# Gate and up of blocks 4 to 14 of a second feed-forward by seven block products, in a hybrid encoder layer on one core

## The chip, the core and the metric

The kernel runs on one core of one Trainium2 chip. The metric is the device time of one execution in microseconds (us); the number before the change is the median of three runs. Engines are called as in the profile: PE (TensorE matmul), PEld (its weight loads), DVE (VectorE), ACT (ScalarE), POOL (GpSimd), SP (SyncE, which here only issues transfers).

## What is computed

One layer of an encoder on 544 tokens (512 of a prompt and 32 of a sample, D = 1024): a feed-forward half step, a mixing stage (retention and sparse attention), and a second feed-forward half step, each closed by a layer norm on a scaled residual. The part that matters is the second feed-forward:

```python
def swiglu(h, w_gate, w_up, w_down):
    a = jnp.einsum('btd,df->btf', h, w_gate)
    u = jnp.einsum('btd,df->btf', h, w_up)
    return jnp.einsum('btf,fd->btd', jax.nn.silu(a) * u, w_down)
...
x = post_norm(x, swiglu(modulate(x, sh3, sc3), f2_gate, f2_up, f2_down), 1.0 + gt3, 0.5, ln3_g, ln3_b)
```

The hidden width is 2816, which is 22 blocks of 128 columns.

## The kernel before, in words

Everything is held transposed: features on the 128 partitions, tokens along the free axis, in two halves of 272 (`HALVES`). All large products run in fp32r with operands split in a high and a low part; `mm3` (line 140) makes three matmuls of one product of tiles: high by high, high by low, low by high. Each matmul is 128x128 weights by 272 columns, recorded under line 75 (`mm`).

A feed-forward block f (`ffn_up`, line 194) takes one gate and one up weight block of [1024, 128], and for each of them and each half of the tokens runs 8 contraction tiles by 3 matmuls into one PSUM bank (`ffn_mm`): 4 x 24 = 96 matmuls. `ffn_act` then makes tanh on ACT (line 188), the gating and the product on DVE (189, 190), the high part of the hidden block on ACT (191) and the low part on DVE (192). Gate halves use three banks of tag "a", up halves two of "l" and two of "t". Blocks 0 and 1 run side by side, contraction tile by contraction tile (`k_outer`), while the normalised input `h` is still being made; blocks 2 to 21 follow one by one.

Weights flow through a list `stream`, made up ahead by `queue_w`. `next_w` keeps three weights (`AHEAD`) split beyond the one in use. For each, `fetch_w` loads 512 KB on SP into one of three buffers `wr`; `split_w` casts the high part on ACT (line 129) into one of five buffers `wh`, writes its negative to the low part on ACT (133), and POOL issues a transfer that adds the weight from DRAM to it (134). With `lo_eng` given, that engine subtracts instead (136).

The order of issue is set by hand where it matters: all PE instructions, and all loads issued through `load`, are chained in program order. `tick()` is called after each product and resumes jobs that were spawned and asked to be resumed so many ticks later; so side work is put into the program at a pace. `tc.keep_in_program_order` pins an instruction's place; other instructions may be moved ahead by the scheduler when their engine is free. Each engine runs its queue in order. SBUF beside weights is one pool of 35 units (`unit`, 128x1088 floats): `h` takes 8, the hidden blocks 22, the residual `xr` 4, the partial sums and weight tiles of the conditioning products the rest.

Two pieces of side work lie beside the second feed-forward. `residual_next` (355) turns the residual into its scaled form: eight multiplies on POOL (359) and eight scalings on ACT (361), spawned before block 2. `cond((8, (2, 3)))` makes the last gate's conditioning vector on DVE: eight loads of 512 KB and sixteen products over 1024 columns (554, 556), one step every 2 or 3 ticks from block 2 on, then `cond_done`. After block 21 the down projection (`proj_residual`) reads the hidden blocks, adds to the residual, and the last layer norm ends the kernel.

Of the kernel before, what the change touches and what calls it, by code (L numbers as in the profile page):

```python
# [9 lines left out]
F32 = mybir.dt.float32  # L10
FR = mybir.dt.float32r
I32 = mybir.dt.int32
AF = mybir.ActivationFunctionType
ALU = mybir.AluOpType
NOSYNC = mybir.DependencyInfo(mybir.DependencyClass.NoSync, mybir.DependencyReason.DATA)

P = 128
D = 1024
ND = D // P
TP = 512  # L20
TS = 32
T = TP + TS
HT = T // 2
FF = 2816
NF = FF // P
# [5 lines left out]
HALVES = ((0, HT), (HT, T))  # L31
SEGS = ((((0, HT), 0),), (((HT, TP), 0), ((TP, T), 1)))
DOWN_G = ((0, 8), (8, 15), (15, 22))
AHEAD = 3


@with_exitstack
def encoder_layer_kernel(ctx, tc, xT, cT, wc1, w_e, w_cond, b_condT, lnp, w_gu1, w_dn1, w_in, w_out, w_gu2, w_dn2,
                         ckT, cv, cikT, s0, cmat, ropes, dec, csm,
                         yT, akT, avT, ikT, st_p, st_s):  # L40
    nc = tc.nc
    ctx.enter_context(nc.allow_low_precision("operands are split exactly into two float32r parts"))
    const = ctx.enter_context(tc.tile_pool(name="const", bufs=1))
    up = ctx.enter_context(tc.tile_pool(name="up", bufs=35))
    wr = ctx.enter_context(tc.tile_pool(name="wr", bufs=3))
    wh = ctx.enter_context(tc.tile_pool(name="wh", bufs=5))
# [4 lines left out]
    def unit(name, dt=F32):  # L51
        return up.tile([P, 2, T], dt, name=name, tag="u")

    def scr(name, shape=None, dt=F32):
        return sp.tile(shape or [P, T], dt, name=name, tag="s", bufs=4)

    def half_scr(name, shape=None):
        return sp.tile(shape or [P, HT], F32, name=name, tag="t", bufs=4)

    def bank(tag, name):  # L60
        return pp.tile([P, 512], F32, name=name, tag=tag, bufs=dict(a=3, l=2, t=2, o=1)[tag])
# [9 lines left out]
    def load(*a):  # L71
        ordered("load", nc.sync.dma_start(*a))

    def mm(*a, **kw):
        ordered("pe", nc.tensor.matmul(*a, **kw))  # L75
# [14 lines left out]
    def spawn(job):  # L90
        resume(job, now[0] + 1)

    def tick():
        now[0] += 1
        due = [j for t, j in jobs if t <= now[0]]
        jobs[:] = [x for x in jobs if x[0] > now[0]]
        for job in due:
            resume(job, now[0])
# [19 lines left out]
    def fetch_w(src, n, name):  # L118
        raw = wr.tile([P, ND, P], F32, name=f"wr_{name}", tag="wr")
        load(raw[:, :n, :], src)  # L120
        return raw

    def split_w(raw, n, name, lo_eng=None, pool=None, pin=False, src=None):
        if pool is None:
            hl = wh.tile([P, 2, ND, P], FR, name=f"wh_{name}", tag="wh")
            hi, lo = hl[:, 0], hl[:, 1]
        else:
            hi, lo = (pool.tile([P, ND, P], FR, name=f"wu_{name}", tag="u") for _ in range(2))
        c = nc.scalar.copy(hi[:, :n, :], raw[:, :n, :])  # L129
        if pin:  # L130
            tc.keep_in_program_order(c)
        if src is not None and lo_eng is None:
            nc.scalar.mul(lo[:, :n, :], hi[:, :n, :].bitcast(F32), -1.0)  # L133
            nc.gpsimd.dma_start(lo[:, :n, :], src, accum_op=ALU.add)  # L134
        else:
            r = (lo_eng or nc.gpsimd).tensor_tensor(lo[:, :n, :], raw[:, :n, :], hi[:, :n, :].bitcast(F32), op=ALU.subtract)
            last["lo"] = r.ins.name
        return hi, lo
# [7 lines left out]

    stream = []
    split = []

    def ensure(n):  # L150
        while len(split) < n and stream:
            src, cnt, kw = stream.pop(0)
            split.append(split_w(fetch_w(src, cnt, "w"), cnt, "w", src=src, **kw))

    def next_w(ahead=AHEAD):
        ensure(1 + ahead)
        return split.pop(0)

    def queue_w(src, n=ND, **kw):
        stream.append((src, n, kw))  # L160
# [12 lines left out]
    def ffn_mm(st, h, which, i, tag=None):  # L173
        hls, banks = st
        if hls[which] is None:
            hls[which] = next_w()
        a, b = HALVES[i]
        ps = bank(tag or ("a" if which == 0 else "lt"[i]), f"gu{which}_{i}")[:, :HT]
        for k in range(ND):
            mm3(ps, hls[which], k, h[k], a, b, k == 0, k == ND - 1)  # L180
        banks[which, i] = ps
        tick()

    def ffn_act(st, hid, i):
        a, b = HALVES[i]
        pg, pu = st[1][0, i], st[1][1, i]
        t = half_scr("tnh")
        nc.scalar.activation(t, pg, AF.Tanh, scale=0.5)  # L188
        nc.vector.scalar_tensor_tensor(t, t, 1.0, pg, op0=ALU.add, op1=ALU.mult)  # L189
        nc.vector.tensor_tensor(t, t, pu, op=ALU.mult)  # L190
        nc.scalar.copy(hid[:, 0, a:b], t)  # L191
        nc.vector.tensor_tensor(hid[:, 1, a:b], t, hid[:, 0, a:b].bitcast(F32), op=ALU.subtract)  # L192

    def ffn_up(h, hid):
        st = [None, None], {}
        for which in range(2):
            for i in range(2):
                ffn_mm(st, h, which, i)
        for i in range(2):
            ffn_act(st, hid, i)  # L200
# [154 lines left out]
    def residual_next(xr, rs, al, j):  # L355

        for i, (a, b) in enumerate(HALVES):
            rb = rs[i].unsqueeze(1).to_broadcast([P, 2, HT])
            tc.keep_in_program_order(nc.gpsimd.tensor_tensor(xr[j][:, :, a:b], xr[j][:, :, a:b], rb, op=ALU.mult))
        for d in (2 * j, 2 * j + 1):  # L360
            tc.keep_in_program_order(nc.scalar.activation(xv(xr, d), xv(xr, d), AF.Identity, bias=al[1][:, d:d + 1],
                                                          scale=al[0][:, d:d + 1]))
# [32 lines left out]
    DN += [(6, *g, 1) for g in ((8, 12), (12, 15), (15, 18), (18, 22))] + [(7, *g, 1) for g in DOWN_G]  # L395
    OUT = [(d, 0, 8, i) for i in range(2) for d in range(ND)]

    def queue_ffn(w_gu, w_dn, f0, first=False):
        for f in range(f0, NF):
            for which in range(2):  # L400
                queue_w(w_gu[f - f0, which], lo_eng=(nc.gpsimd, nc.vector)[which] if first and f == f0 else None,
                        pin=first and 2 * (f - f0) + which < AHEAD)
        for d in range(ND):
            for k0, k1 in DOWN_G:
                queue_w(w_dn[d][:, k0:k1, :], k1 - k0)

    queue_ffn(w_gu1, w_dn1, 2, True)
    for c in range(4):
        queue_w(w_in[c], lo_eng=nc.gpsimd if c else nc.vector, pool=up)
    for c in [4] + [17 + hh + 4 * j for hh in range(4) for j in range(3)] + [  # L410
# [5 lines left out]
        queue_w(w_gu2[0, which], pool=up)  # L416
    queue_w(w_gu2[1, 0])
    queue_w(w_gu2[1, 1], pool=up)
    queue_ffn(w_gu2[2:], w_dn2, 2)


    xr = [unit(f"xr{j}") for j in range(4)]
    h = new_h("h1_")
# [61 lines left out]
    for d in range(ND):  # L485
# [17 lines left out]
        x = xv(xr, d)  # L503
        for i in range(2):
            a0, b0 = HALVES[i]
            f = half_scr("hf")
            for (a, b), r in SEGS[i]:
                nc.vector.tensor_scalar(f[:, a - a0:b - a0], x[:, a:b], g1[:, r, d:d + 1], modT[:, r, d:d + 1],
                                        op0=ALU.mult, op1=ALU.add)
# [6 lines left out]
    for n in range(len(ACC)):  # L516
        catch_up(n, ND)
    ensure(AHEAD)
    onesr = const.tile([P, P], FR, name="onesr")
# [24 lines left out]
    def cond(*parts):  # L544
        n = 0
        for m, pace in parts:
            acc = [up.tile([P, 1024], F32, name=f"ca{m}_{r}", tag="u") for r in range(2)]
            for d in range(ND):
                w = up.tile([P, 1024], F32, name=f"wc{m}_{d}", tag="u")
                load(w, w_cond[d * P:(d + 1) * P, 1024 * m:1024 * m + 1024])  # L550
                for r in range(2):
                    c = cz[:, d, r:r + 1]
                    if d == 0:
                        nc.vector.tensor_scalar(acc[r], w, c, None, op0=ALU.mult)
                    else:
                        nc.vector.scalar_tensor_tensor(acc[r], w, c, acc[r], op0=ALU.mult, op1=ALU.add)  # L556
                n += 1
                yield pace[n % len(pace)]
            spawn(cond_done(m, acc))
# [11 lines left out]
    hid = []  # L571
# [14 lines left out]
    al2 = alpha_ln(2, lp[:, 2, :], lp[:, 3, :])  # L586
    G2, B2 = mod_consts(2, 3, 4, lp[:, 0, :], lp[:, 1, :])

    h, rs, fin = ln_to_h(xr, G2, B2, "h2_", 4, 1)
# [6 lines left out]
    xd = nc.dram_tensor("x_spill", [4, P, 2 * T], F32, kind="Internal").ap()  # L596
# [547 lines left out]
    for hh in range(4):  # L1144
        mixed[hh] = unit("mx", FR)
        if hh == 0:
            xr = [unit(f"xq{j}") for j in range(4)]
# [4 lines left out]
        def gated(ps, a, b):  # L1152
            t = half_scr("rgt")
            nc.scalar.activation(t, ps, AF.Tanh, scale=0.5)
            nc.vector.scalar_tensor_tensor(t, t, 1.0, ps, op0=ALU.add, op1=ALU.mult)
            nc.vector.tensor_mul(t, t, rt[:, a:b])
            mixed_part(hh, t, a, b)
# [6 lines left out]
    h, rs, fin = ln_to_h(xr, G3, B3, "h3_", 3, 4)  # L1164
# [2 lines left out]

    hid = [unit("hid", FR), unit("hid", FR)]
    sts = [([next_w(0), next_w(0)], {}) for f in range(2)]
    for i in range(2):  # L1170
        for f in range(2):
            for which in range(2):
                sts[f][1][which, i] = bank(("aaao", "lltt")[i][2 * f + which], "gu_e")[:, :HT]
        k_outer([(sts[f][0][w], sts[f][1][w, i]) for f in range(2) for w in range(2)], h, i)
        for f in range(2):
            ffn_act(sts[f], hid[f], i)

    def residual():
        yield 2
        for j in range(4):  # L1180
            residual_next(xr, rs, al2, j)
            yield 1

    spawn(residual())
    for f in range(2, NF):
        hid.append(unit("hid", FR))
        ffn_up(h, hid[f])
        if f == 2:
            spawn(cond((8, (2, 3))))
    known(8)  # L1190
    C3 = gate_coef(3, 8, 0.25)

# [146 lines left out]
```

## Time and profile before

| | |
|---|---|
| median of 3 runs | 1190.45 us (1190.23 to 1190.97) |
| profiled execution | 1189.48 us |
| its span, first to last instruction | 1187.4 us |
| mean granted clock of PE | 0.991 |
| PE busy | 1159.3 us, 98% |
| DVE, ACT, POOL busy | 56%, 49%, 17% |
| matmuls under line 75 of gate and up (both feed-forwards, from block 2) | 3840, 482.7 us |

The second feed-forward's blocks 0 and 1 end at 798.56 us in the span, blocks 2 to 21 at about 1039 us, and the down projection and the norm take the rest. In rows of the profile, `out<-in` are the program's names of what is written and read, the figure behind the count is the busy time in us and the next the mean of one in ns; behind the second bar stands the idle time of the engine ahead of them and what ended it. In rows of the chain and of the timeline the first two numbers are start and length in us.

### The profile page before, as it was taken

What the parts mean: (1) busy time and instruction counts of PE and PEld (TensorE: products, weight loads), DVE (VectorE), ACT (ScalarE), POOL (GpSimd) and SP (SyncE); (2) the same over time, 40 slices, a digit from 0 to 9 for tenths busy, and PEclk for the clock granted to TensorE, in tenths of its full rate; (3) what the DMA queues carried; (4) which work ended last, traced back from release to release, by engine and by line L of the source; (5) the groups of instructions that cost most, each with busy time, mean ns of one, the idle gap of its engine ahead of it and who ended that gap; (6) DMA issues with size and microseconds to landing.
All of it is one profiled execution on the core that took longest, in us unless ns stands there. A gap on an engine that the chain in (4) does not pass through costs nothing.

```text
span 1187.4 us, 23002 instructions
## 1 busy us (share of the span) xinstructions
PE 1159.3 (98%) x9419; PEld 1127.8 (95%) x9419; DVE 665.8 (56%) x1574; ACT 586.7 (49%) x990; POOL 199.7 (17%) x231
## 2 busy tenths in 40 slices
PE   9999999999999999899989999999999999999995
PEld 7999999999999999789979989999999999999995
DVE  5767665764468484677887775885542222201416
ACT  3644444444335364655466577546444444433423
POOL 0112111111111303312111101104111111111110
PEclk9999999999999999999989999999999999999998
DMA  9899999997999466644845588807988878788842
GB/s 359 293 297 308 239 256 229 258 215 183 296 259 215 119 222 168 149 116 115 193 100 162 132 257 225 209 31 197 263 177 175 177 175 173 163 173 176 177 88 76
DMA packets 71451, 231.41 MB, mean 195 GB/s; under 512 B 8657, under 2 KB 12881, under 8 KB 71345
## 3 DMA queue, kind: packets, MB, share of 16 engines
q0 software_dynamic: 23472, 83.37, 40.3%
q1 hardware_dynamic: 47728, 146.43, 35.5%
q8 instruction: 74, 1.21, 0.4%
q14 instruction: 33, 0.26, 0.1%
q10 hardware_dynamic: 144, 0.14, 0.0%
HBM read 220.54 MB, written 7.35 MB: 192 GB/s over the span
## 4 chain that ended last, share of the span: by engine, by line
PE 89%; DVE 4%; DMA 4%; ACT 2%; issue 1%; SPq 0%; DVEq 0%; ACTq 0%
PE gu L75 40%; PE dn L75 26%; PE in L75 15%; DMA we_raw<-in_w_e 3%; PE gu_e L75 2%; PE po L75 1%; PE pt L78 1%; DMA wh_w<-in_w_gu 1%; PE ro L75 1%; PE lg L75 1%; PE isc L75 1%; ACT wh_w L129 0%; DMA cm<-in_cmat 0%; DVE wk L804 0%; ACT wh_w L133 0%
## 5 line engine op out<-in xcount | busy, mean ns | idle before, releaser
L75 PE MATMUL gu<-h,wh_w 128*128 128x272 f32 x3840 | 482.7, 288 | 0.6 <-DMA wh_w<-in_w_gu 0.6
L75 PEld LDWEIGHTS gu<-h,wh_w 128*128 128x128 f32 x3840 | 481.4, 188 | 0.8 <-DMA wh_w<-in_w_gu 0.8
L75 PE MATMUL dn<-hid,wh_w 128*128 128x272 f32 x2112 | 266.6, 288 | 0.0
L75 PEld LDWEIGHTS dn<-hid,wh_w 128*128 128x128 f32 x2112 | 265.4, 188 | 0.2
L129 ACT CAST wh_w<-wr_w 128x1024 fp32r<-128x1024 f32 (+1 forms) x162 | 165.6, 1024 | 152.9 <-PE dn L75 102.1
L75 PE MATMUL in<-h,wh_w 128*128 128x272 f32 x1392 | 189.9, 294 | 0.0
L75 PEld LDWEIGHTS in<-h,wh_w 128*128 128x128 f32 x1392 | 179.6, 191 | 5.3 <-issue 3.4
L133 ACT ACTIVATE wh_w<-wh_w 128x1024 fp32r<-128x1024 f32 (+1 forms) x158 | 163.7, 1037 | 2.9
L556 DVE SCALAR_TENSOR_TENSOR ca<-wc,cz,ca 128x1024 f32<-128x1024 f32 x98 | 129.7, 1349 | 26.5 <-DMA wc<-in_w_cond 26.2
L134 POOL DMA_DIRECT2D wh_w<-in_w_gu x79 | 69.2, 876 | 408.8 <-ACT wh_w L133 333.6
L190 DVE TENSOR_TENSOR tnh<-tnh,gu 128x272 f32<-128x272 f32 x80 | 35.0, 437 | 123.1 <-PE gu L75 123.1
L188 ACT ACTIVATE tnh<-gu 128x272 f32<-128x272 f32 x80 | 31.8, 397 | 112.9 <-PE gu L75 112.7
L189 DVE SCALAR_TENSOR_TENSOR tnh<-tnh,gu 128x272 f32<-128x272 f32 x80 | 34.7, 435 | 84.3 <-ACT tnh L188 84.1
L191 ACT CAST hid<-tnh 128x272 fp32r<-128x272 f32 x88 | 36.7, 418 | 88.9 <-DVE tnh L190 88.9
L134 POOL DMA_DIRECT2D wh_w<-in_w_dn x48 | 41.7, 870 | 224.7 <-ACT wh_w L133 215.4
L270 DVE SCALAR_TENSOR_TENSOR xq<-dn,C,xq 128x272 f32<-128x272 f32 (+2 forms) x48 | 18.0, 404 | 105.2 <-PE dn L75 105.2
L192 DVE TENSOR_TENSOR hid<-tnh,hid 128x272 fp32r<-128x272 f32 x88 | 40.7, 464 | 39.2 <-ACT hid L191 38.2
L134 POOL DMA_DIRECT2D wh_w<-in_w_in x29 | 25.3, 885 | 136.2 <-ACT Pu L964 30.9
L803 DVE MAX8 m<-wk 128x8 f32<-128x544 f32 (+3 forms) x65 | 38.8, 598 | 0.7
L804 DVE MATCH_REPLACE8 wk<-m,wk 128x544 f32<-128x544 f32 (+3 forms) x65 | 38.0, 584 | 0.0
L75 PE MATMUL gu_e<-h,we 128*128 128x272 f32 x192 | 27.3, 296 | 0.5 <-ACT h L510 0.4
L75 PEld LDWEIGHTS gu_e<-h,we 128*128 128x128 f32 x192 | 24.8, 188 | 2.4 <-issue 1.0
(266 smaller groups left out, 1103.1 us busy)
## 6 DMA issues: line engine op xcount, KB each, us to landing
wr_w<-in_w_gu SPq DMA_DIRECT2D x84, 512.0 KB, 5.5
wh_w<-in_w_gu POOLq DMA_DIRECT2D x79, 512.0 KB, 7.3
wc<-in_w_cond SPq DMA_DIRECT2D x56, 512.0 KB, 6.9
wr_w<-in_w_in SPq DMA_DIRECT2D x33, 512.0 KB, 5.3
wh_w<-in_w_in POOLq DMA_DIRECT2D x29, 512.0 KB, 6.8
wr_w<-in_w_dn SPq DMA_DIRECT2D x32, 448.0 KB, 4.0
wh_w<-in_w_dn POOLq DMA_DIRECT2D x32, 448.0 KB, 5.4
wc<-in_wc SPq DMA_DIRECT2D x16, 512.0 KB, 8.0
```

Source lines behind the costliest of these rows:

```text
L75: ordered("pe", nc.tensor.matmul(*a, **kw))
L129: c = nc.scalar.copy(hi[:, :n, :], raw[:, :n, :])
L133: nc.scalar.mul(lo[:, :n, :], hi[:, :n, :].bitcast(F32), -1.0)
L134: nc.gpsimd.dma_start(lo[:, :n, :], src, accum_op=ALU.add)
L188: nc.scalar.activation(t, pg, AF.Tanh, scale=0.5)
L189: nc.vector.scalar_tensor_tensor(t, t, 1.0, pg, op0=ALU.add, op1=ALU.mult)
L190: nc.vector.tensor_tensor(t, t, pu, op=ALU.mult)
L191: nc.scalar.copy(hid[:, 0, a:b], t)
L192: nc.vector.tensor_tensor(hid[:, 1, a:b], t, hid[:, 0, a:b].bitcast(F32), op=ALU.subtract)
L556: nc.vector.scalar_tensor_tensor(acc[r], w, c, acc[r], op0=ALU.mult, op1=ALU.add)
L803: behind(nc.vector.max(m8, w), "pe")
L804: nc.vector.match_replace(w, in_to_replace=m8, in_values=w, imm_value=MARK)
```

## The change

Blocks 4 to 14 (`SEVEN`) of the second feed-forward are computed as a 2 by 2 block product with seven products instead of eight. The weights of a block form [gate; up] by the two halves of the contraction (a11, a12, a21, a22); the activations form the two halves of the contraction by the two halves of the tokens. Each of the seven products has four contraction tiles and one token half: 12 matmuls.

- `activation_sums` makes, once, four combinations of the activation blocks (8 units `hs`, split in high and low) beside blocks 0 to 2.
- `seven` runs one block. TensorE's order in it: C; a product onto A, after which `s2` is copied out; B; a product onto A, after which `s4` is copied out; the first product of the next block (`begin`, into its own A, copied out as `s1`); a last product onto A; a last one onto B. Sums that standard form would add on DVE are chained in PSUM: A and B are added to further while the copies hold the intermediate sums.
- weights: high and low of the gate block and of the second half of the up block as before (`make_gate`, `make_up`); DVE makes four sums of weight blocks in place in the raw buffers (`weight_sums`), and `split_sums` splits them (cast on ACT, subtraction on DVE). All of that for the next blocks, in pinned order; the snapshots (`snapshot`) are pinned too.
- the hidden block is finished one block later (`finish_block`).
- the residual is stored to DRAM in block 3 (`put_by`, through the ordered `load`), loaded again after block 19 (`bring_back`) and scaled then; the conditioning moves to after block 15, a step every 1 or 2 ticks.
- `stream` gets a stop (`None`) ahead of block 4, and `fetch_ahead` starts loads apart from splits. In blocks 15 to 21 DVE makes the low part of the gate weights (of block 15 both).

```diff
+SEVEN = (4, 14)
...
+                    elif not first and (f == SEVEN[1] + 1 or f > SEVEN[1] and which == 0):
+                        eng = nc.vector
...
+            elif f == SEVEN[0]:
+                stream.append(None)
...
+    sums = [unit("hs", FR) for _ in range(ND)]
+
+    def activation_sums():
+        yield 0
+        for k in range(4):
+            ta, tb = sums[k], sums[4 + k]
+            la, lb = scr("la"), scr("lb")
+            for x, l in ((h[k], la), (h[4 + k], lb)):
+                nc.vector.tensor_tensor(l, x[:, 0].bitcast(F32), x[:, 1].bitcast(F32), op=ALU.add)
+            for o, p, q in ((la[:, 0:HT], la[:, HT:T], la[:, 0:HT]), (la[:, HT:T], lb[:, HT:T], la[:, HT:T]),
+                            (lb[:, HT:T], lb[:, HT:T], la[:, 0:HT]), (lb[:, 0:HT], lb[:, 0:HT], lb[:, HT:T])):
+                nc.vector.tensor_tensor(o, p, q, op=ALU.subtract)
+            for x, l in ((ta, la), (tb, lb)):
+                nc.scalar.copy(x[:, 0], l)
+                nc.vector.tensor_tensor(x[:, 1], l, x[:, 0].bitcast(F32), op=ALU.subtract)
+            yield 2
+
     for i in range(2):
+        if i:
+            spawn(activation_sums())
...
-    def residual():
-        yield 2
+    def put_by():
+        yield 6
         for j in range(4):
-            residual_next(xr, rs, al2, j)
+            load(xd[j], xr[j].rearrange("p a t -> p (a t)"))
+
+    def bring_back():
+        yield 0
+        xs = [unit(f"xs{j}") for j in range(4)]
+        for j in range(4):
+            load(xs[j].rearrange("p a t -> p (a t)"), xd[j])
+        yield 3
+        for j in range(4):
+            residual_next(xs, rs, al2, j)
             yield 1
...
+    def negated(hi, lo, src):
+        pin(nc.scalar.mul(lo, hi.bitcast(F32), -1.0))
+        nc.gpsimd.dma_start(lo, src, accum_op=ALU.add)
...
+    def weight_sums(f):
+        a11, a12, a21, a22 = (r[f][:, s] for r in (raw_g, raw_u) for s in (LO, HI))
+        for o, x, y, op in ((a22, a21, a22, ALU.add), (a21, a11, a21, ALU.subtract), (a11, a22, a11, ALU.subtract),
+                            (a12, a12, a11, ALU.subtract)):
+            pin(nc.vector.tensor_tensor(o, x, y, op=op))
+
+    def split_sums(f, W, raw):
+        W[f] = wh.tile([P, 2, ND, P], FR, name="wh_s", tag="wh")
+        pin(nc.scalar.copy(W[f][:, 0], raw[f]))
+        pin(nc.vector.tensor_tensor(W[f][:, 1], raw[f], W[f][:, 0].bitcast(F32), op=ALU.subtract))
+
+    def product(ps, W, w0, act, k0, i, start, stop):
+        a, b = HALVES[i]
+        for k in range(4):
+            for n, (x, y) in enumerate(((0, 0), (0, 1), (1, 0))):
+                mm(ps, W[:, x, w0 + k, :], act[k0 + k][:, y, a:b], start=start and not k and not n,
+                   stop=stop and k == 3 and n == 2, skip_group_check=True)
...
+    def finish_block(n):
...
+            if n == 0:
+                pin(nc.vector.tensor_tensor(t, t, u, op=ALU.mult))
+            elif n == 1:
+                pin(nc.scalar.copy(hid[:, 0], flat))
+            else:
+                pin(nc.vector.tensor_tensor(hid[:, 1], flat, hid[:, 0].bitcast(F32), op=ALU.subtract))
...
+    def seven(f, hid):
...
+        if f + 2 <= last7:
+            make_gate(f + 2)
...
+        C = bank("l", "pC")[:, :HT]
+        product(C, Wg[f], 4, h, 4, 0, True, True)
+        pin(nc.vector.tensor_tensor(u[:, 0], s1.pop(f), C, op=ALU.add))
+        finish_block(0)
+        pin(nc.scalar.activation(t[:, 0], u[:, 0], AF.Tanh, scale=0.5))
+        gated(t[:, 0], u[:, 0])
+        if more:
+            make_up(f + 1, 0)
+        tick()
+        product(A[f], Wg2[f], 0, sums, 4, 1, False, True)
+        s2 = snapshot(A[f], "s2")
+        if more:
+            weight_sums(f + 1)
+            make_up(f + 1, 1)
+        finish_block(1)
+        B = bank("t", "pB")[:, :HT]
+        product(B, Wu2[f], 0, sums, 0, 1, True, True)
+        tick()
+        product(A[f], Wu2[f], 4, sums, 0, 0, False, True)
+        s4 = snapshot(A[f], "s4")
+        pin(nc.vector.tensor_tensor(u[:, 1], s4, B, op=ALU.add))
+        if more:
+            begin(f + 1)
+            split_sums(f + 1, Wg2, raw_g)
+            s1[f + 1] = snapshot(A[f + 1], "s1")
+        else:
+            ensure(len(split) + 1)
+            ffn_mm(plain, h, 0, 0)
+        finish_block(2)
+        tick()
+        product(A[f], Wg2[f], 4, h, 4, 1, False, True)
+        if more:
+            split_sums(f + 1, Wu2, raw_u)
+        pin(nc.scalar.activation(t[:, 1], A[f], AF.Tanh, scale=0.5))
+        gated(t[:, 1], A.pop(f))
+        product(B, Wu[f], 0, sums, 4, 0, False, True)
+        pin(nc.vector.tensor_tensor(u[:, 0], s2, B, op=ALU.add))
+        pending.append((t, u, hid))
...
+        if f == last7 + 1:
+            spawn(cond((8, (1, 2))))
+        if f == 19:
+            spawn(bring_back())
```

More of the change, by code (lines that the diff above doesn't have):

```diff
@@ L148, in encoder_layer_kernel, with fetch_ahead @@
     split = []
+    fetched = []
+    def fetch_ahead():
+        src, cnt, kw = stream[len(fetched)]
+        fetched.append(fetch_w(src, cnt, "w"))
     def ensure(n):
-        while len(split) < n and stream:
+        while len(split) < n and stream and stream[0]:
+            if not fetched:
+                fetch_ahead()
             src, cnt, kw = stream.pop(0)
-            split.append(split_w(fetch_w(src, cnt, "w"), cnt, "w", src=src, **kw))
+            split.append(split_w(fetched.pop(0), cnt, "w", src=src, **kw))
     def next_w(ahead=AHEAD):
@@ L396, in encoder_layer_kernel, with queue_ffn @@
     OUT = [(d, 0, 8, i) for i in range(2) for d in range(ND)]
[L398 to L402, printed above, removed]
+    def queue_ffn(w_gu, w_dn, first):
+        for f in range(2, NF):
+            if first or not SEVEN[0] <= f <= SEVEN[1]:
+                for which in range(2):
+                    eng = None
+                    if f == 2 and first:
+                        eng = (nc.gpsimd, nc.vector)[which]
+                    elif not first and (f == SEVEN[1] + 1 or f > SEVEN[1] and which == 0):
+                        eng = nc.vector
+                    queue_w(w_gu[f - 2 if first else f, which], lo_eng=eng, pin=first and 2 * f + which < 4 + AHEAD)
+            elif f == SEVEN[0]:
+                stream.append(None)
         for d in range(ND):
@@ L405, in queue_ffn @@
                 queue_w(w_dn[d][:, k0:k1, :], k1 - k0)
-    queue_ffn(w_gu1, w_dn1, 2, True)
+    queue_ffn(w_gu1, w_dn1, True)
     for c in range(4):
@@ L418, in encoder_layer_kernel @@
     queue_w(w_gu2[1, 1], pool=up)
-    queue_ffn(w_gu2[2:], w_dn2, 2)
+    queue_ffn(w_gu2, w_dn2, False)
     xr = [unit(f"xr{j}") for j in range(4)]
@@ L1176, in encoder_layer_kernel @@
             ffn_act(sts[f], hid[f], i)
-    def residual():
-        yield 2
+    def put_by():
+        yield 6
         for j in range(4):
-            residual_next(xr, rs, al2, j)
-            yield 1
-    spawn(residual())
+            load(xd[j], xr[j].rearrange("p a t -> p (a t)"))
[7 more added lines that the diff above has]
+            residual_next(xs, rs, al2, j)
+            yield 1
+        back.extend(xs)
@@ new lines, in encoder_layer_kernel, with load_gate, load_up, make_gate @@
+    back = []
+    pin = tc.keep_in_program_order
+    LO, HI = slice(0, 4), slice(4, 8)
+    raw_g, raw_u, Wg, Wu, Wg2, Wu2 = {}, {}, {}, {}, {}, {}
+    def load_gate(f):
+        raw_g[f] = fetch_w(w_gu2[f, 0], ND, "g")
+    def load_up(f):
+        raw_u[f] = up.tile([P, ND, P], F32, name="wr_u", tag="u")
+        load(raw_u[f], w_gu2[f, 1])
+    def negated(hi, lo, src):
+        pin(nc.scalar.mul(lo, hi.bitcast(F32), -1.0))
+        nc.gpsimd.dma_start(lo, src, accum_op=ALU.add)
+    def make_gate(f):
+        Wg[f] = wh.tile([P, 2, ND, P], FR, name="wh_g", tag="wh")
+        pin(nc.scalar.copy(Wg[f][:, 0], raw_g[f]))
+        negated(Wg[f][:, 0], Wg[f][:, 1], w_gu2[f, 0])
@@ new lines, in make_up @@
+    def make_up(f, n):
+        if n == 0:
+            Wu[f] = up.tile([P, 2, 4, P], FR, name="wh_u", tag="u")
+            pin(nc.scalar.copy(Wu[f][:, 0], raw_u[f][:, HI]))
+        else:
+            negated(Wu[f][:, 0], Wu[f][:, 1], w_gu2[f, 1][:, HI])
+    def weight_sums(f):
[3 more added lines that the diff above has]
+            pin(nc.vector.tensor_tensor(o, x, y, op=op))
@@ new lines, in snapshot, with begin @@
+    def snapshot(ps, name):
+        s = half_scr(name)
+        pin(nc.scalar.copy(s, ps))
+        return s
+    first7, last7 = SEVEN
+    A, s1 = {}, {}
+    def begin(f):
+        A[f] = bank("a", "pA")[:, :HT]
+        product(A[f], Wg[f], 0, h, 0, 0, True, True)
+    pending = []
+    def finish_block(n):
+        if pending:
+            t, u, hid = pending[0]
+            flat = t.rearrange("p a t -> p (a t)")
+            if n == 0:
+                pin(nc.vector.tensor_tensor(t, t, u, op=ALU.mult))
[3 more added lines that the diff above has]
+                pin(nc.vector.tensor_tensor(hid[:, 1], flat, hid[:, 0].bitcast(F32), op=ALU.subtract))
+                pending.clear()
@@ new lines, in gated @@
+    def gated(t, g):
+        pin(nc.vector.scalar_tensor_tensor(t, t, 1.0, g, op0=ALU.add, op1=ALU.mult))
+    def seven(f, hid):
+        t, u = scr("tnh", [P, 2, HT]), scr("up", [P, 2, HT])
+        more = f < last7
+        if f + 2 <= last7:
+            make_gate(f + 2)
+        else:
+            ensure(len(split) + 1)
+        if f + 3 <= last7:
+            load_gate(f + 3)
+        else:
+            fetch_ahead()
+        if f + 2 <= last7:
+            load_up(f + 2)
+        C = bank("l", "pC")[:, :HT]
[23 more added lines that the diff above has]
+            s1[f + 1] = snapshot(A[f + 1], "s1")
+        else:
+            ensure(len(split) + 1)
+            ffn_mm(plain, h, 0, 0)
[9 more added lines that the diff above has]
+        pending.append((t, u, hid))
+        if not more:
+            for n in range(3):
+                finish_block(n)
+        tick()
@@ L1185, in encoder_layer_kernel, with pass_bar @@
+    plain = [None, None], {}
+    def pass_bar():
+        assert stream.pop(0) is None
+    spawn(put_by())
     for f in range(2, NF):
         hid.append(unit("hid", FR))
-        ffn_up(h, hid[f])
-        if f == 2:
-            spawn(cond((8, (2, 3))))
+        if f == first7 - 2:
+            load_gate(first7)
+            load_up(first7)
+        if f == first7 - 1:
+            load_gate(first7 + 1)
+            load_up(first7 + 1)
+            load_gate(first7 + 2)
+        if first7 <= f <= last7:
+            if f == first7:
+                pass_bar()
+            seven(f, hid[f])
+            continue
+        st = plain if f == last7 + 1 else ([None, None], {})
+        for which in range(2):
+            for i in range(2):
+                if (which, i) not in st[1]:
+                    ffn_mm(st, h, which, i)
+                if f == first7 - 1:
+                    if which == 0 and i == 0:
+                        make_gate(first7)
+                        make_up(first7, 0)
+                        make_up(first7, 1)
+                    if which == 0 and i == 1:
+                        weight_sums(first7)
+                    if which == 1 and i == 0:
+                        split_sums(first7, Wg2, raw_g)
+                        split_sums(first7, Wu2, raw_u)
+                        make_gate(first7 + 1)
+        for i in range(2):
+            ffn_act(st, hid[f], i)
+        if f == first7 - 1:
+            begin(first7)
+            s1[first7] = snapshot(A[first7], "s1")
+        if f == last7 + 1:
+            spawn(cond((8, (1, 2))))
+        if f == 19:
+            spawn(bring_back())
@@ L1190, in encoder_layer_kernel @@
+    xr = back
+    assert len(xr) == 4
     known(8)
```

## The prediction

> **What bounds the kernel now.** I read the totals first, then the chain that ended last in order of time, then the second feed-forward stretch by stretch.
>
> ```profile
> span 1187.4 us, 23002 instructions
> PE 1159.3 (98%) x9419; PEld 1127.8 (95%) x9419; DVE 665.8 (56%) x1574; ACT 586.7 (49%) x990; POOL 199.7 (17%) x231
> L75 PE MATMUL gu<-h,wh_w 128*128 128x272 f32 x3840 | 482.7, 288 | 0.6 <-DMA wh_w<-in_w_gu 0.6
> ```
>
> ```profile
> 786.46 12.10 PE gu_e L75 x95
> 798.56 102.22 PE gu L75 x816
> 900.95 138.33 PE gu L75 x1104
> 1039.29 69.15 PE dn L75 x552
> ```
>
> TensorE is the bound: from 798.56 us to the end of the gate and up products the chain holds nothing but matmuls, 816 + 1104 = 1920 in 240.55 us, 125.3 ns each. (One matmul's record lasts 288 ns; the next starts 125 ns later, so a result stands some 0.16 us behind the last start.) A block of 128 hidden columns is 96 matmuls, 12.03 us. The other engines have room there:
>
> ```profile
> core 0: us, PE busy (x) PEld busy (x) DVE busy (x) ACT busy (x) POOL busy (x), PEclk, DMA share, GB/s
> 906.00:930.00 24.00, 24.00 (x193) 24.00 (x193) 5.28 (x12) 11.08 (x16) 3.48 (x4) 1.00 0.82 175
> ```
>
> Over two blocks VectorE is busy 5.28 of 24 us, ScalarE 11.08, and the granted clock is 1.00. A matmul taken out of this stage shortens the path by 125.3 ns, as long as nothing else takes TensorE's place.
>
> **The products.** In blocks 4 to 14 gate and up become seven products of 12 matmuls (4 contraction tiles by 3 split terms, same 272 columns): 84 in place of 96, 10.53 us in place of 12.03. Removed: 11 x 12 x 125.3 ns = **16.54 us**. Nothing else can shorten the path, since the stage held no idle TensorE time to win.
>
> **What a block adds on the other engines.** Rows for the same or the nearest shapes:
>
> ```profile
> L190 DVE TENSOR_TENSOR tnh<-tnh,gu 128x272 f32<-128x272 f32 x80 | 35.0, 437 | 123.1 <-PE gu L75 123.1
> L189 DVE SCALAR_TENSOR_TENSOR tnh<-tnh,gu 128x272 f32<-128x272 f32 x80 | 34.7, 435 | 84.3 <-ACT tnh L188 84.1
> L461 DVE TENSOR_TENSOR we<-we_raw,we 128x512 fp32r<-128x512 f32 x8 | 5.5, 692 | 8.6 <-ACT we L460 8.6
> L136 DVE TENSOR_TENSOR wu_w<-wr_w,wu_w 128x1024 fp32r<-128x1024 f32 x3 | 3.7, 1226 | 1.9 <-ACT wu_w L129 1.9
> L306 DVE TENSOR_TENSOR xr<-xr,lnm 128x544 f32<-128x544 f32 x6 | 4.3, 717 | 0.0
> L129 ACT CAST wh_w<-wr_w 128x1024 fp32r<-128x1024 f32 x130 | 135.6, 1045 | 83.0 <-PE dn L75 38.5 <-PE gu L75 35.7 <-DMA wr_w<-in_w_gu 6.6
> L133 ACT ACTIVATE wh_w<-wh_w 128x1024 fp32r<-128x1024 f32 x126 | 133.3, 1059 | 2.2
> L460 ACT CAST we<-we_raw 128x512 fp32r<-128x512 f32 x8 | 5.0, 622 | 1.4 <-DMA we_raw<-in_w_e 1.1
> L613 ACT COPY aqk<-in 128x272 f32<-128x272 f32 x16 | 6.1, 382 | 18.2 <-PE in L75 17.8
> L188 ACT ACTIVATE tnh<-gu 128x272 f32<-128x272 f32 x80 | 31.8, 397 | 112.9 <-PE gu L75 112.7
> L134 POOL DMA_DIRECT2D wh_w<-in_w_gu x79 | 69.2, 876 | 408.8 <-ACT wh_w L133 333.6 <-ACT hid L191 50.4 <-DVE lnz L317 12.6
> ```
>
> VectorE: three half-width adds (3 x 0.437), two gatings (2 x 0.435), the product and the low part of hid over 544 columns (2 x 0.717), four weight sums over 512 (4 x 0.692), two low parts of summed weights (2 x 1.226): 1.31 + 0.87 + 1.43 + 2.77 + 2.45 = 8.83 us of 10.53. ScalarE: three casts of 1024 (3.14), one negation of 1024 (1.06), a cast and a negation of 512 (1.24, both taken at 0.622), three snapshots (1.15), two tanh (0.79), the hid cast over 544 columns (0.65, between the 512 and the 1024 row): 8.03 us. POOL issues two accumulating transfers, as before. By sums all fit; the order decides.
>
> I lay the pinned order on a clock that starts with the product C of block f. TensorE's seven products end at 1.50, 3.01, 4.51, 6.01, 7.52, 9.02 and 10.53; a result is readable 0.16 later. ScalarE comes out of block f-1's last tanh at 9.58 of that block and takes the cast and negation of Wg(f+2), to 1.16 of this one. C is added to s1 on VectorE 1.66 to 2.10, the tanh follows to 2.50, the half cast for up to 3.12, then **snapshot s2** 3.17 to 3.55. The product A4 overwrites that accumulator from 4.51: slack 0.96. Negation and hid cast end at 4.81; **s4** runs 6.17 to 6.55 and is wanted at 7.52: slack 0.97. The cast of Wg2 ends at 7.60, s1 of the next block at 8.06, the cast of Wu2 at 9.11, the tanh of A at 9.58, which closes the loop. VectorE: product of block f-1 to 2.82, gating to 3.25, weight sums to 6.02, the add of s4 and B 6.55 to 6.99 (B is written again from 9.02), the low part of Wg2 to 8.83 (read 3.2 us later), hid to 9.55, the low part of Wu2 to 10.78 (read at 3.01 of the next block, 2.8 us later), gating and last add to 11.65, that is 1.12 of the next block, where its first work comes at 1.66. So no wait of TensorE remains in the steady state; the least cover is 0.96 us, on two snapshots. If it is gone, each microsecond of lateness beyond it costs 11 us in all. **I take 0**, with ends 0 and 0.5 us a block (5.5 us).
>
> **The transfers.**
>
> ```profile
> wr_w<-in_w_gu SPq DMA_DIRECT2D x84, 512.0 KB, 5.5
> wh_w<-in_w_gu POOLq DMA_DIRECT2D x79, 512.0 KB, 7.3
> wc<-in_wc SPq DMA_DIRECT2D x16, 512.0 KB, 8.0
> x_spill<-xr SPq DMA_DIRECT2D x4, 544.0 KB, 6.5
> ```
>
> A block moves 1.75 MB in place of 2 (the accumulating half for up is 256 KB). Raw gate weights sit in three buffers: one comes free at 8.83, its load lands 5.5 later, and ScalarE's cast wants it 11.28 after the release: slack 5.8 us. The accumulating transfers have over 10 us against 7.3. The residual's four stores go on SP's queue in block 3, behind the loads of gates 5 and 6; weights are ahead by a block, so 4 x 544 KB cost nothing. On the way back (block 20) four loads of the same size precede the reads by three products, 9 us, and POOL's eight multiplies and ScalarE's eight scalings move with them, to a stretch where both engines have as much room as in the row from 906 us. The multiplies go ahead of the down weights' transfers on POOL, which are three weights (over 15 us) early. I take 0, ends 0 and 1.
>
> **The way in.** This is where I see a price. The activation sums are four steps of VectorE work, each four operations over 544 columns and four over 272, with two casts on ScalarE between, put into the program before the activations of blocks 0 and 1 (second half) and of block 2.
>
> ```profile
> 767.27 2.63 DVE L227 TENSOR_TENSOR xq<-xq,shc 128x544 f32<-128x544 f32 x4
> 771.05 0.44 DVE L248 TENSOR_TENSOR S<-S,xq 128x272 f32<-128x272 f32 x1
> 771.40 0.44 DVE L236 TENSOR_TENSOR Q<-Q,sq 128x272 f32<-128x272 f32 x1
> 795.01 0.79 DVE L192 TENSOR_TENSOR hid<-tnh,hid 128x272 fp32r<-128x272 f32 x2
> ```
>
> Back to back, operations start 0.64 us apart at 544 columns ((2.63 - 0.72) / 3) and 0.35 at 272, so a step is 4 x 0.64 + 4 x 0.35 = 3.96 and the four 15.8 us. VectorE is solidly busy until 795.80. Sums and the six-by-two activations of the second half (2 x 3 x 0.35 = 2.1) end at 795.8 + 17.9 = 813.7, and block 2's gating, which frees the first of the three gate banks, at 814.1. TensorE wants that bank for the second gate half of block 3, 120 matmuls after 798.56: 813.6. A stall of 0.5 us, more if VectorE waits for ScalarE's casts inside the steps: at worst 1 us in each step, 4.5 in all. I take **1.0**, nearer the low end, since other ready work can fill those waits. Gone from this stretch, with no gain to the path, are the conditioning products and POOL's multiplies.
>
> **The way out.** After block 14 the conditioning for the last gate runs at one step in 1.5 products in place of 2.5, and VectorE makes one low part in two weights.
>
> ```profile
> 177.20 54.17 PE gu L75 x432
> L556 DVE SCALAR_TENSOR_TENSOR ca<-wc,cz,ca 128x1024 f32<-128x1024 f32 x98 | 129.7, 1349 | 26.5 <-DMA wc<-in_w_cond 26.2
> ```
>
> Eight steps of two at 1.35 in three blocks are 21.6, with 3 x 2.6 for the activations and 3 x 1.23 for the low parts 33 of 36 us. In the first feed-forward such steps came every 2.25 products and TensorE kept 125.4 ns a matmul (432 in 54.17). Here a step can lie just ahead of an activation: bank freed 2.7 + 0.4 us after the block, wanted at 3.0. I take **0.5**, ends 0 and 3.
>
> **A rule that speaks against it.** VectorE has the least room, so I looked at what stretches it.
>
> ```profile
> 814.49 8.27 DVE L556 SCALAR_TENSOR_TENSOR ca<-wc,cz,ca 128x1024 f32<-128x1024 f32 x2
> 816.06 5.60 POOL L359 TENSOR_TENSOR xq<-xq,lny 128x544 f32<-128x544 f32 x4
> 838.48 2.48 DVE L556 SCALAR_TENSOR_TENSOR ca<-wc,cz,ca 128x1024 f32<-128x1024 f32 x2
> 839.45 0.87 POOL L134 DMA_DIRECT2D wh_w<-in_w_gu x1 [7.09 <-ACT wh_w L133]
> ```
>
> Two VectorE operations that take 2.48 us took 8.27 beside POOL's multiplies, but 2.48 with a transfer issue of POOL inside them. In the seven-product blocks POOL has issues alone, so VectorE keeps its 8.83. If issues did hold it for their length, 2 x 0.876 would make it 10.58, 0.05 over the block: 0.6 us in all. The Trainium skill, "SBUF — State Buffer", section "Who interferes with whom", says that a VectorE instruction with two SBUF inputs contends with a GpSimd instruction that reads SBUF. The row with the multiplies agrees; read to cover issues too, the rule would give the 0.6 us worse, and the last two rows speak against that.
>
> **Sum.** 16.5 - 1.0 - 0.5 = 15.0 us less. The profiled execution took 1189.48 (2.1 us outside its span) and would take 1174.5; the median of the runs is 0.97 above it, which gives **1175.4**. With this case's own bounds it runs from 1173.9 (nothing lost) to 1179.
>
> **Rivals.** *A wait in every block* (18%): a snapshot or low part comes late, because the real order on ScalarE or VectorE differs from mine. For it: three quarters of ScalarE and five sixths of VectorE are used, in fixed order, and each waits for the other several times a block. Against: 0.96 us of cover. At 0.3 to 0.8 us a block 3.3 to 8.8 us go, 1178.7 to 1184.
>
> *Slower* (5%): ScalarE's queue stands behind a late gate load. The cast of Wg(f+2) heads the queue, with the tanh and s2 behind it and A4 behind s2. A landing time over 11.28 + 0.96 = 12.2 us holds TensorE; over 13.7 it takes back all 1.50 us of a block. At 14.5 us the kernel is 0.8 x 11 = 8.8 us slower, 1199. Against: the slowest median for a load of that size is 8.0 us, in the crowded start.
>
> *Nothing gained* (3%): these waits come to about 1.5 us a block, or the ways in and out cost ten times what I took, 1189 to 1192.
>
> **Numbers.** The forecast as costed has 74%. Faster by over 0.2% (2.4 us, about what can be told from no change) are the forecast and the wait in every block: 0.92; within 0.2% 0.03, slower 0.05. The range goes from 1173.2 (all saved, less the runs' spread) to 1183, into the second case.
>
> **What would show it.** Right: 132 fewer matmuls; blocks 4 to 14 as one stretch of TensorE work of 924 matmuls in about 116 us; a gap of about 1 us near block 3's second gate half; VectorE over 80% busy in the stretch and ScalarE about 76%. Wrong: TensorE waiting for ScalarE (snapshots) or for VectorE (low parts) eleven times; ScalarE's cast waiting for gate loads; a gap in blocks 16 to 18 behind the conditioning products; a matmul spacing other than 125 ns in products of twelve.

## The result, and the profile after

The changed kernel takes 1196.89 us (median; 1195.92 to 1201.4) against 1190.45 before: ratio 1.0064, 95% interval [1.004, 1.0088]. It is slower, by 6.4 us; 15.0 us less were forecast. Two executions among the experiments were far slower than their like and are left out of the medians and ratios: one of 2848.62 us with the up load behind, which is the one that its trace holds, so that no row of this kernel is shown, and one of 1199.28 us with the repeated casts. The page of the changed kernel's profiled execution (1201.4 us, the slowest of five):

```profile
span 1199.6 us, 22951 instructions
PE 1148.6 (96%) x9287; PEld 1115.7 (93%) x9287; DVE 757.0 (63%) x1691; ACT 605.3 (50%) x1034; POOL 192.8 (16%) x223
```

The 132 matmuls are gone (9419 to 9287) and TensorE is busy 10.7 us less, yet the span is longer: TensorE waits where it did not before. What it waited for in the second feed-forward (engine, line, releaser; us in total, times, longest), from the list of waits:

```profile
PE gu L76 <- ACT wh_w L130: 11.8, 1, 11.8
PE gu L76 <- DMA wh_w<-in_w_gu: 8.3, 1, 8.3
```

Two waits, both in block 2, which is computed as before, ahead of all that is new on TensorE. None is in the seven-product blocks. Their stretch of the chain, one block and the start of the next (start, us, what):

```profile
862.85 1.49 PE pC L76 x12
864.35 1.50 PE pA L76 x12
865.85 1.50 PE pB L76 x12
867.34 4.52 PE pA L76 x36
871.86 1.49 PE pB L76 x12
873.35 1.49 PE pC L76 x12
```

From one C to the next 10.50 us; 10.53 were forecast. The engines over 20 us, nearly two such blocks (windows, columns as in the prediction):

```profile
880.00:900.00 20.00, 20.00 (x162) 20.00 (x162) 16.27 (x26) 14.34 (x23) 3.43 (x4) 1.00 0.74 179
```

VectorE 81%, ScalarE 72%, TensorE without a gap, clock 1.00. So the change does what it says in its main part, and the loss sits on the way in. There SP's queue, from the timeline, tells the first half of the story:

```profile
728.01 7.11 SPq L73 DMA_DIRECT2D wr_w<-in_w_gu  x4
736.92 0.33 SPq L73 DMA_DIRECT2D wr_g<-in_w_gu  x1
774.95 0.33 SPq L73 DMA_DIRECT2D wr_u<-in_w_gu  x1
775.37 42.37 SPq L73 DMA_DIRECT2D wr_w<-in_w_gu  x4
```

The last four `wr_w` are the weights of blocks 2 and 3. In the kernel before they came directly behind the first four:

```profile
722.92 33.27 SPq L72 DMA_DIRECT2D wr_w<-in_w_gu  x9
```

Now the gate and up loads of block 4 stand ahead of them. The up load goes into one of the 35 units, gets none until 774.95, and every load behind it in the chain stands for 38 us. What released it, by the list of SP's own waits, is a matmul of the output projection (`dn`):

```profile
SPq L73 <- PE dn L76: 37.6, 1, 37.6
```

At that time this projection reads weights that are held in units (timeline):

```profile
771.73 6.14 PE L76 MATMUL dn<-mx,wu_w 128*128 128x272 f32 x48
```

The second half of the story is ScalarE's queue, where the casts now come late (changed kernel, timeline):

```profile
813.77 0.65 ACT L1198 CAST hs<-la 128x544 fp32r<-128x544 f32 x1 [2.54 <-DVE la L1196]
814.32 1.04 ACT L130 CAST wh_w<-wr_w 128x1024 fp32r<-128x1024 f32 x1
815.41 0.82 PE L76 MATMUL gu<-h,wh_w 128*128 128x272 f32 x2 [11.77 <-ACT wh_w L130]
816.86 0.86 POOL L135 DMA_DIRECT2D wh_w<-in_w_gu  x1 [70.24 <-DVE la L1196]
824.54 25.67 PE L76 MATMUL gu<-h,wh_w 128*128 128x272 f32 x185 [8.30 <-DMA wh_w<-in_w_gu]
```

The load of the first raw weight was issued at 775.37 and landed within 5.3 us, but its cast stands behind the casts of the activation sums, which wait for VectorE. TensorE wanted it at 803.6, got the high part 11.8 us later, ran two matmuls, and waited 8.3 us more for the low part, which is a negation, a POOL issue and a transfer further. So the weight lay landed for some 33 us. From the start of its cast to the low part it is 10.2 us (814.32 to 824.54); by this estimate a cast at landing would have had both parts ready at about 791, in time for 803.6. It is the cast's place in ScalarE's queue that holds TensorE, and the load order acts through that place; why the program is built with the casts so far behind no row shows. In the kernel before this cast ran at 750.86, during the output projection:

```profile
750.86 1.04 ACT L129 CAST wh_w<-wr_w 128x1024 fp32r<-128x1024 f32 x1 [1.75 <-PE dn L75]
```

A third piece hangs on the wait. The 190 matmuls after it took 26.30 us, where 125.3 ns each make 23.8. The windows show why (the column ahead of the DMA share is the granted clock):

```profile
824.00:826.00 2.00, 1.46 (x6) 1.46 (x7) 0.00 (x0) 1.30 (x2) 0.00 (x0) 0.50 1.06 274
828.00:830.00 2.00, 2.00 (x12) 2.00 (x11) 0.00 (x0) 0.17 (x1) 0.52 (x1) 0.62 1.03 270
830.00:832.00 2.00, 2.00 (x18) 2.00 (x17) 0.44 (x1) 0.23 (x1) 0.00 (x0) 1.00 1.05 324
```

TensorE came back from the wait at half its clock for 5.0 us, until about 829.5 (0.62 on average from 828 to 830 is 0.50 for 1.5 us and 1.00 for the rest): 2.5 us lost. The bill from the first plain gate block to the down projection: 240.73 us before (798.56 to 1039.29) and 247.0 after (803.65 to 1050.67), 6.3 more; and - 16.5 + 20.1 + 2.5 = 6.1.

### The profile page after: what moved, and what is told of

Its sections match the earlier page's. It is cut to its first block, busy times and chain, and to the rows that moved or that the text cites. A ratio compares the mean times of both kernels' runs of the same rounds, so it can differ in the third digit from the quotient of the medians.

```text
span 1199.6 us, 22951 instructions
## 1 busy us (share of the span) xinstructions
PE 1148.6 (96%) x9287; PEld 1115.7 (93%) x9287; DVE 757.0 (63%) x1691; ACT 605.3 (50%) x1034; POOL 192.8 (16%) x223
## 4 chain that ended last, share of the span: by engine, by line
PE 83%; issue 6%; DMA 5%; DVE 3%; ACT 1%; SPq 0%; POOL 0%; DVEq 0%; ACTq 0%; POOLq 0%
PE gu L76 29%; PE dn L76 23%; PE in L76 14%; PE pA L76 6%; PE pB L76 3%; DMA we_raw<-in_w_e 3%; PE pC L76 1%; PE po L76 1%; PE pt L79 1%; PE ro L76 1%; DMA wh_w<-in_w_gu 1%; PE lg L76 1%; PE isc L76 1%; DMA rp<-iqf 1%; PE gu_e L76 0%
## 5 line engine op out<-in xcount | busy, mean ns | idle before, releaser
L76 PE MATMUL gu<-h,wh_w 128*128 128x272 f32 x2784 | 353.4, 289 | 20.1 <-ACT wh_w L130 11.8
L76 PEld LDWEIGHTS gu<-h,wh_w 128*128 128x128 f32 x2784 | 351.7, 189 | 20.6 <-ACT wh_w L130 12.0
L130 ACT CAST wh_w<-wr_w 128x1024 fp32r<-128x1024 f32 (+1 forms) x140 | 142.8, 1022 | 120.0 <-PE dn L76 95.2
L134 ACT ACTIVATE wh_w<-wh_w 128x1024 fp32r<-128x1024 f32 (+1 forms) x128 | 132.1, 1033 | 2.5
L135 POOL DMA_DIRECT2D wh_w<-in_w_gu x49 | 42.9, 876 | 328.5 <-ACT wh_w L134 242.2
L199 ACT CAST hid<-tnh 128x272 fp32r<-128x272 f32 x66 | 27.5, 419 | 90.4 <-DVE tnh L198 90.4
L198 DVE TENSOR_TENSOR tnh<-tnh,gu 128x272 f32<-128x272 f32 x58 | 25.3, 437 | 75.1 <-PE gu L76 75.1
L197 DVE SCALAR_TENSOR_TENSOR tnh<-tnh,gu 128x272 f32<-128x272 f32 x58 | 24.9, 434 | 34.6 <-ACT tnh L196 34.5
L76 PE MATMUL pA<-hs,wh_s 128*128 128x272 f32 x264 | 36.6, 288 | 0.0
L76 PEld LDWEIGHTS pA<-hs,wh_s 128*128 128x128 f32 x264 | 34.4, 188 | 0.0
```

## The experiments

Theory A: the up load of block 4 stands in the load chain and waits for a unit; the weights of blocks 2 and 3 come late, and their casts then fall behind those of the activation sums. Rival B: the activation sums by themselves keep VectorE and ScalarE from the casts. The lines of the change at issue, which the core of the diff above leaves out:

```diff
     for f in range(2, NF):
         hid.append(unit("hid", FR))
...
+        if f == first7 - 2:
+            load_gate(first7)
+            load_up(first7)
...
             for i in range(2):
...
                     ffn_mm(st, h, which, i)
```

`ffn_mm` asks for block 2's weights and three more, so their loads come into the program after these two.

**The four weights first.**

```diff
         if f == first7 - 2:
+            ensure(1 + AHEAD)
             load_gate(first7)
             load_up(first7)
```

> The four weights of blocks 2 and 3 are fetched and split ahead of the loads of gate and up of block 4; nothing else differs from the changed kernel (1196.9 us, with waits of TensorE of 11.8 and 8.3 us in block 2). Theory A (the load of up of block 4 waits for a free unit and holds the weights of blocks 2 and 3 behind it in the load chain; their casts then stand behind those of the activation sums): both waits go, 1196.9 - 20.1 = 1176.8, up to 1180 if the sums still delay block 3. Rival B (VectorE's and ScalarE's work on the activation sums holds the casts up whatever the load order): at least 10 us of waits in block 2 stay, 1187 or more.

Measured: 1178.6 us against 1189.97 in the same set, ratio 0.9904, interval [0.9889, 0.9919]. Moving two loads behind four turns the change from slower to 11.4 us faster; both waits in block 2 are gone. B, which expected 1187 or more, falls as the whole cause. One wait is left on the way in:

```profile
PE pA L76 <- DMA wh_g<-in_w_gu: 2.3, 2, 1.9
```

The longer, 1.9, is for the low part of block 4's gate weight, whose cast stands behind the sums' casts as well; the other is for block 5's.

**The sums four products later, load order kept.** The spawn of `activation_sums` moves from the second half of blocks 0 and 1 to the start of block 2.

```diff
-        if i:
-            spawn(activation_sums())
...
     spawn(put_by())
+    spawn(activation_sums())
```

> Load order as in the changed kernel, but the activation sums are put into the program four products later (beside blocks 2 and 3). Theory A: the weights still arrive late, and the first cast stands behind the first step of the sums, at about 804 us in the span: some 1 us of wait for the high part and 8 to 10 for the low part stay, 1186 to 1188. Rival B: no wait, 1177.

Measured: 1187.14, ratio 0.9974, interval [0.9963, 0.9985]. The waits:

```profile
PE gu L76 <- DMA wh_w<-in_w_gu: 9.1, 2, 8.2
PE gu L76 <- ACT wh_w L130: 2.2, 1, 2.2
```

As A has it, with 2.2 for the high part where about 1 stood. Of the 9.1 us 0.8 lie in the first feed-forward; in block 2 it is 8.2 and 2.2. So 10.4 of the 20.1 us of waits stay, and 9.7 went with the sums' casts, of which now one stands ahead of the first weight's cast in place of five. That cast came at 801.22, though its load had been issued at 765.75: what stays is a place in the queue too.

**Only the gate load moved, and only the up load moved.** The first:

```diff
         if f == first7 - 2:
-            load_gate(first7)
             load_up(first7)
         if f == first7 - 1:
+            load_gate(first7)
```

> Only the gate load of block 4 is moved behind the four weights; the up load stays ahead of them. Theory A (it is the up load's wait for a unit): the load chain stands until about 775 us as before and the waits stay, 1195 to 1198. If instead the gate load is the cause, by taking one of the three raw buffers: the waits go, 1177 to 1180.

The second is its complement (`load_up(first7)` moves instead).

> The complement of the kernel with the up load first: only the up load of block 4 is moved, to block 3, the gate load stays ahead of the four weights. Theory A (the up load's wait for a unit blocks the chain): the waits of 20 us go, 1177 to 1180, like the kernel with the four weights first. If the gate load's hold on one of three raw buffers mattered: a wait of several us before block 3, 1182 or more.

Measured: with the up load in front 1196.7, ratio 1.0067, interval [1.0047, 1.0088], and the same waits as in the changed kernel:

```profile
PE gu L76 <- ACT wh_w L130: 11.8, 1, 11.8
PE gu L76 <- DMA wh_w<-in_w_gu: 8.7, 2, 8.0
```

With the up load behind 1177.67, ratio 0.9901, interval [0.9884, 0.9917]. So it is the load that needs a unit, and not the one that takes a raw buffer. With the up load in front its wait ends with the same releaser as in the changed kernel, a matmul of the output projection, after 39.5 us; the unit it got had, by that, held a weight of this projection.

**The casts ahead of the sums' casts, load order kept.** The loads and the four splits are put into the program ahead of block 0, and each cast of the sums is ordered behind the last split:

```diff
+    load_gate(SEVEN[0])
+    load_up(SEVEN[0])
+    ensure(1 + AHEAD)
     for i in range(2):
         if i:
             spawn(activation_sums())
...
-                nc.scalar.copy(x[:, 0], l)
+                r = nc.scalar.copy(x[:, 0], l)
+                tc.add_manual_dep(r.ins, last["cast"], NOSYNC, reason="order of issue")
```

> Load order as in the changed kernel (up of block 4 ahead of the four weights) and the sums where they were, but the four casts of blocks 2 and 3 stand ahead of the sums' casts in ScalarE's queue. Theory A: the raw weights land at about 781 us, are cast at about 782, low parts land at about 792, TensorE wants them at 804: no wait, 1177 to 1180. If the late load alone were enough to make the wait: 5 us or more stay, 1182 or more. Rival B: at least 10 us stay, 1187 or more.

Measured: 1183.61, ratio 0.9945, interval [0.9929, 0.996], by the number the second case (1182 or more). But the kernel was not the test I meant. Put into the program that early, the up load got a unit at once, so the chain did not stand for it (timelines of SP and ScalarE, and the waits):

```profile
733.62 0.38 SPq L73 DMA_DIRECT2D wr_u<-in_w_gu  x1
736.17 51.67 SPq L73 DMA_DIRECT2D wr_w<-in_w_gu  x4
```

```profile
795.44 1.04 ACT L130 CAST wh_w<-wr_w 128x1024 fp32r<-128x1024 f32 x1 [3.89 <-DMA wr_w<-in_w_gu]
796.39 0.32 ACT L360 ACTIVATE h<-ht,B 128x32 fp32r<-128x32 f32 x1
```

```profile
PE gu_e L76 <- ACT h L360: 7.7, 2, 5.7
```

The early gate load held one of three raw buffers, so the third and fourth weights' loads waited for the casts of the first two (784.43 and 786.46), and the fourth's cast, now far ahead in ScalarE's queue, held the activations of `h` behind it: another wait of 7.7 us, in blocks 0 and 1. It speaks against B only as far as VectorE goes (no wait in block 2 with the sums in their old place), and says nothing of a late load alone. It does show that an early load does not by itself make an early cast: the first weight's load was issued at 736.17, its cast came at 784.43.

**The gate weight of block 4 a block earlier.** On top of the four weights first:

```diff
                 if f == first7 - 1:
                     if which == 0 and i == 0:
-                        make_gate(first7)
                         make_up(first7, 0)
...
+                if f == first7 - 2 and which == 1 and i == 0:
+                    make_gate(first7)
```

> The kernel with the four weights first (1178.6), and the gate weight of block 4 cast and negated one block earlier. Theory: the two waits of TensorE for that weight's low part (2.3 us in the kernel with the four weights first) go, 1176.3. If something else sets the start of block 4 (VectorE behind the activation sums): the wait stays at 1 to 2 us under another name, 1177.5 to 1178.6.

Measured: 1175.67 against 1188.78, ratio 0.9888, interval [0.9872, 0.9903]: 13.1 us faster than before, the lowest median here, with no wait of the new products left in the list. Its expectation of 1176.3 holds. Beside the kernel with the four weights first (0.9904, another set) the intervals overlap; that the 2.3 us went is read from the waits.

**How much cover the snapshot has.** Two casts repeated on ScalarE ahead of s2, on top of the four weights first:

```diff
+        if f + 2 <= last7:
+            pin(nc.scalar.copy(Wg[f + 2][:, 0], raw_g[f + 2]))
+            pin(nc.scalar.copy(Wu[f + 1][:, 0], raw_u[f + 1][:, HI]))
         s2 = snapshot(A[f], "s2")
```

> The kernel with the four weights first, and in blocks 4 to 12 two casts are repeated on ScalarE ahead of snapshot s2 (128x1024 and 128x512, 1.6 us), which changes no value. Theory (the clock of a block: s2 has 0.9 us of cover before TensorE needs the accumulator): TensorE waits for the snapshot, (1.6 - 0.9) = 0.6 to 0.7 us in nine blocks, 5.5 to 6.5 us more than 1178.6. If there is more cover than that (buffers, or another order): no change, 1178.6.

Measured: 1182.99, ratio 0.9945, interval [0.9929, 0.9962]: by the two ratios 0.41% or 4.9 us above the kernel it is built on. In the chain one C follows the other after 11.02 to 11.06 us in place of 10.50, some 0.53 in each of the eight blocks behind block 4, and TensorE waits for the snapshot in nine:

```profile
849.63 1.53 PE pC L76 x12
860.68 1.53 PE pC L76 x12
```

```profile
PE pA L76 <- ACT s L1276: 3.5, 9, 1.3
```

The longest, 1.3, is block 4's; the other eight are some 0.27 each, and the 36 matmuls right behind such a wait take some 4.76 us in place of 4.52, which is the rest of the 0.53.

Without the casts s2 begins at 884.82 and A is written again from 886.11 (timelines of the kernel with the four weights first):

```profile
884.82 0.39 ACT L1276 COPY s<-pA 128x272 f32<-128x272 f32 x1
886.11 1.67 PE L76 MATMUL pA<-hs,wh_s 128*128 128x272 f32 x12
```

Cover 0.90 us. Back to back the two casts take 1.47 us (0.95 + 0.52, by the next starts) and not the 1.6 of their durations, which makes 0.57 a block where 0.6 to 0.7 were expected: that is why the expectation was too high.

**The kernel before, again.**

> The kernel before, once more, for a second profile of the stages ahead of the second feed-forward, whose instructions stand in the same order in all kernels. If the 0.2 to 5.1 us by which the changed kernels enter the output projection later are spread between executions: this profile differs from the first by up to some us there as well. If they belong to the changed program: it agrees with the first within 0.5 us.

```profile
725.84 3.02 PE dn L75 x24
803.21 102.22 PE gu L75 x816
905.60 138.33 PE gu L75 x1104
```

Measured: one execution, 1194.26. The gate products begin 4.65 us later than in the first profile (798.56) and then run alike. It enters its output projection at 725.84, 4.5 us later. So of the 5.1 us by which the profiled execution of the changed kernel does so (726.47 against 721.38) 4.5 lie within what one and the same kernel shows between executions; the seven-product change is not needed to explain them. Whether the changed program adds the other 0.6 stays open.

## Why the prediction was wrong, point by point

- **Products: right.** 132 matmuls gone, 10.50 us a block where 10.53 stood.
- **The order inside a block: right**, nearly to the tenth. The prediction's timetable put s2 1.67 us behind its product C's end; the trace of the kernel with the four weights first has C beginning at 881.63 and s2 at 884.82, 3.19 after the block's start where 3.17 was worked out. Cover 0.90 for 0.96, and the repeated casts show that it is real. The low parts of the weight sums, with VectorE at 81%, held nothing up.
- **The rule on VectorE and GpSimd: as taken.** VectorE's operations with two SBUF inputs kept their length beside POOL's issues (in the kernel with the four weights first a weight sum took 0.69 us from 886.22 inside an issue of 0.86 from 886.14; 0.692 stood), so the 0.6 us stayed out. The Trainium skill, "SBUF — State Buffer", section "Who interferes with whom", and the trace agree if an issue is not counted as an instruction that reads SBUF.
- **The transfers: the failed step.** The prediction said that the residual's stores go behind the loads of gates 5 and 6 and that "weights are ahead by a block". It counted buffers and landing times in the steady state and never asked where the first gate and up loads of block 4 stand: in the chain ahead of the weights of blocks 2 and 3, with a target from another pool. That is 20.1 us of waits and 2.5 of half clock against 0 taken. With this and the cast below put right the kernel is 13.1 us faster, where 15.0 were forecast.
- **The way in: right place, wrong size and mechanism.** VectorE's queue with the sums was costed for the bank it frees in block 3, 1.0 us. With the load order mended the price is 2.3 us, and by ScalarE: casts of weights behind casts of the sums. The same oversight, that what is in the program later can stand behind the sums in the queue, was worth 9.7 of the 20.1 us in the changed kernel.
- **The upper end.** The ends named for the terms (5.5, 1, 4.5 and 3 us) add up to 14 us, which is 1187.9 from 1173.9; the 1179 given is not their sum. The end that the failed step broke is the 1 us of the transfers.
- **The way out: right.** No wait in blocks 15 to 21 (600 matmuls in 75.15 us); the 0.5 was not needed.
- **The rivals.** The slower one had the shape (ScalarE's queue behind a late load) but in the wrong place: in each block with a landing time, where it was once, before the blocks, behind a load that had stood unissued for 38 us. Its condition, over 13.7 us from request to landing, was looked up against landing times from issue alone.

## What to carry to other kernels

In a chain of loads that is ordered by hand, put ahead of a load only loads whose targets are free by then: a prefetch into a scarcer pool can hold up what is needed sooner. When a change moves a fetch, list the whole queue around it, and for each entry the buffer it waits for, before costing the steady state. And look where the steps behind a moved load end up in their engine's queue: here the first weight had landed some 33 us before its cast, which stood behind other work, and 2.5 us more went because TensorE's granted clock had fallen in the wait.

## What the runs showed of the hardware

TensorE's granted clock fell to 0.50 some 2 us after its last matmul ahead of the waits of 20 us (it ended at 803.65; 0.65 on average from 805.5 to 806, 0.50 after that). Behind them it was 0.50 until about 829.5 us, 5.0 us from the first matmul at 824.54, then 1.00, which cost 2.5 us on top of the waits. The Trainium skill, "TensorE: Matmul & The Clock Gate", Part 1, says that the clock is halved after an idle window and comes back after some 3.4 us of sustained work; the trace agrees in kind, with 5.0 here. The same instructions ahead of the second feed-forward took up to 4.65 us more in another execution of the unchanged kernel.
